# Two value projections run block by block as x arrives, with 1/rms applied after the projections

## The chip, the cores and the metric

The kernel runs on one core of a Trainium2 chip. The time is device microseconds for one execution, the median of several runs. The core has five engines that run side by side, each with its own instruction queue in a fixed order: TensorE (PE, matrix products into PSUM, with its weight loads shown apart as PEld), VectorE (DVE), ScalarE (ACT), GpSimd (POOL), and SyncE (SP), which issues most of the DMAs. Data moves from device memory to SBUF by DMA; PE reads SBUF and writes PSUM, which has eight banks of 128 x 512 float32.

## What is computed

One layer of a streaming encoder on x (512 x 1024, float32): a token mixer, cross-attention into 256 memory tokens, and a SwiGLU. Each has an RMSNorm before and after. The change touches only the first norm and the projections that read it:

```python
h = rms_norm(x, g_mix_pre[l])            # x * rsqrt(mean(x*x) + EPS) * g
proj = h @ w_in[l]                       # 1024 -> 3*512 + 8 + 3*512
q_f, k_f, v_f, f_logit, q_c, k_c, v_c = jnp.split(proj, splits, axis=-1)
log_f = jax.nn.log_sigmoid((f_logit + b_fgate[l]).astype(jnp.float32))
o_f = fox_attention(...)                 # 8 heads of 64, causal, with forget gates
o_c = chunked_rel_attention(...)         # 8 heads of 64, banded, with a learned bias
```

The factor 1/rms belongs to a row of x (a token), the gain g to a column. So the product of (x * g) with the weights, multiplied by the token's 1/rms afterwards, is the same projection.

## The kernel before

**Precision.** Every float32 matrix product is made of three products in a reduced format (fp32r). Each operand is split into hi (rounded by a ScalarE cast or activation) and lo (the rest, by a VectorE subtraction), and `mm3` (L137) adds hi x hi, hi x lo and lo x hi in PSUM.

**Weights.** All weights come through a list of units. A unit is a block of columns of one matrix (mostly 1024 x 256). `load_unit` (L97) issues its DMAs on SP into `raw` tiles (3 buffers), casts hi on ScalarE (L113), and subtracts lo on VectorE (L120) or, for three of four row blocks of the second half, on GpSimd (L116). There are two hi and two lo buffers. `unit()` (L130) hands out the next unit and starts the load of the one behind it.

**Opening.** x comes transposed (features on partitions) in 8 blocks of 128 features. `first_products` (L254) runs as pieces of the first unit (value columns of the second group of fox heads and the 8 forget logits, 264 columns) arrive, piece sizes 1, 1, 2, 2, 2 blocks: for each block it makes hTh and hTl from x * g (L266, L267) and issues 12 products into four PSUM banks `acc0`. It also squares x (L256) and adds up the squares (L258 on GpSimd, L262 and L263 on VectorE). `feature_rstd` (L235) sums them over partitions on PE (L239), takes the power -1/2 (L144, L145), and spreads it over a row of PSUM (L246): `rcol` has 1/rms per token as a column, `rrow` as a row. The four accumulators of the first value unit are copied to V with the factor `rcol` (`raw_v`, L286). Then the second value unit is projected from the same hTh and hTl, 8 blocks x 4 row tiles x 3 products (L305 to L312), and copied in the same way.

**Rescaling h.** While that second projection runs, L314 to L319 make the normalised h for all others: per block xs = x * g * rrow (L315, VectorE, reading rrow from PSUM), hTh again (L318, ScalarE), hTl again (L319, VectorE).

**Heads.** Four groups of four heads follow (two fox, two chunked). `group_proj` (L357) projects a group's values (the first two are there already, in `first_v`), queries and keys. `proj_blocks` (L339) makes two blocks of 128 columns x 512 tokens each; `fin_q` (L376) and `fin_k` (L390) split each block from PSUM into hi and lo for single heads. `head` (L479) is the attention of one head: scores on PE, a row minimum of the negated biased scores on VectorE (L492), exponential on ScalarE (L502), scaling (L503, L504), transposes on PE (L507), hi and lo of the result (L509, L510), and the product with V (L516). Projections of the next group and weight work of later stages lie between the steps of a head on PE; the order on each engine is fixed at build time by a planner that goes by program order, shifted by `later(n)`.

**PSUM.** The banks are shared by tags: a (3), s (2), t (2), o (1). `acc0` takes s, s, a, o; the second value projection takes a, a; statistics take t.

Of the kernel before, what the change touches and what calls it, by code (L numbers as in the profile page):

```python
# [8 lines left out]
F32 = mybir.dt.float32  # L9
F32R = mybir.dt.float32r  # L10
# [23 lines left out]
def hybrid_block_kernel(  # L34
# [44 lines left out]
    def gcol(c):  # L79
        return gn[:, c : c + 1]  # L80
# [16 lines left out]
    def load_unit(w, k0, nkb, c0, ncol, dst=None, sizes=None, after=None):  # L97
        u = len(loaded)
        if dst is None:
            hi = wp.tile([P, nkb, ncol], F32R, tag="hi", name=f"hi{u}", bufs=2)  # L100
            lo = wp.tile([P, nkb, ncol], F32R, tag="lo", name=f"lo{u}", bufs=2)
        else:
            hi, lo = dst()
        step = nkb if nkb * ncol <= 1024 else 4 if ncol < 512 else 2
        j = 0
        for n in sizes or [min(step, nkb - k) for k in range(0, nkb, step)]:
            raw = wp.tile([P, n, ncol], F32, tag="raw", name=f"raw{u}_{j}", bufs=3)
            r0 = (k0 + j) * P
# [4 lines left out]
            act.copy(hi[:, j : j + n, :], raw)  # L113
            pk = 0 if j == 0 or not 2 <= u < 26 else 3 if ncol == 256 else 2 if u >= 20 else 0
            if pk:
                pool.tensor_tensor(  # L116
                    out=lo[:, j : j + pk, :], in0=raw[:, :pk, :], in1=f32(hi[:, j : j + pk, :]), op=ALU.subtract
                )
            if pk < n:
                dve.tensor_tensor(  # L120
                    out=lo[:, j + pk : j + n, :], in0=raw[:, pk:, :], in1=f32(hi[:, j + pk : j + n, :]), op=ALU.subtract
                )
# [101 lines left out]
    with tc.tile_pool(name="mix", bufs=1, reuse_waits="tile") as bp:  # L224
# [3 lines left out]
        warm = small(1, "warm")  # L228
        act.activation(warm, ones, AF.Square)
        acc0 = [bank(tag) for tag in ("s", "s", "a", "o")]  # L230

        def load_x(k, n):
            nc.sync.dma_start(xt[:, k : k + n, :], x_t[k * P : (k + n) * P, :].rearrange("(k p) n -> p k n", p=P))

        def feature_rstd(sq, blocks, n, name):  # L235
            ss = bank("t")
# [11 lines left out]
                )  # L248
            return r, rb[:, : n * P]

        pieces = (1, 1, 2, 2, 2)
        stats = []

        def first_products(hi, lo, k0, n):  # L254
            def squares():
                act.activation(xs[:, k0 : k0 + n, :], xt[:, k0 : k0 + n, :], AF.Square, scale=1.0 / 32.0)  # L256
                for k in range(max(k0, 1), min(k0 + n, KB - 2)):
                    pool.tensor_tensor(out=xs[:, 0, :], in0=xs[:, 0, :], in1=xs[:, k, :], op=ALU.add)  # L258

            if k0 + n == KB:  # L260
                squares()
                dve.tensor_tensor(out=xs[:, KB - 2, :], in0=xs[:, KB - 2, :], in1=xs[:, KB - 1, :], op=ALU.add)  # L262
                dve.tensor_tensor(out=xs[:, 0, :], in0=xs[:, 0, :], in1=xs[:, KB - 2, :], op=ALU.add)  # L263
                stats.append(feature_rstd(xs, (0,), NT, "rx"))
            for k in range(k0, k0 + n):
                act.activation(hTh[:, k, :], xt[:, k, :], AF.Copy, scale=gcol(G_MIX + k))  # L266
                dve.scalar_tensor_tensor(  # L267
                    out=hTl[:, k, :], in0=xt[:, k, :], scalar=gcol(G_MIX + k), in1=f32(hTh[:, k, :]),
                    op0=ALU.mult, op1=ALU.subtract,
                )  # L270
                for t in range(NT):
                    ts = slice(t * P, (t + 1) * P)
                    mm3(acc0[t][:, :264], hTh[:, k, ts], hTl[:, k, ts], hi[:, k, :], lo[:, k, :], k == 0, k == KB - 1)
            if k0 + n < KB:
                load_x(k0 + n, 2 if k0 else 1)
                squares()

        load_x(0, 1)
        load_unit(*units[0], sizes=pieces, after=first_products)

        rcol, rrow = stats[0]

        def v_tile(name):
            return bp.tile([P, NT, 4, 128], F32R, tag="V", name=f"V{name}", bufs=2)
# [11 lines left out]
        for t in range(NT):  # L296
# [6 lines left out]
        acc1 = [bank("a"), bank("a")]  # L303
        load_unit(*units[1])
        for k in range(KB):  # L305
            for t in range(NT):
                ts = slice(t * P, (t + 1) * P)
                mm3(
                    acc1[t // 2][:, (t % 2) * 256 : (t % 2 + 1) * 256], hTh[:, k, ts], hTl[:, k, ts],
                    loaded[1][0][:, k, :], loaded[1][1][:, k, :],  # L310
                    k == 0 and t % 2 == 0, k == KB - 1 and t % 2 == 1,
                )  # L312
        used[0] = 2
        for k in range(KB):  # L314
            dve.scalar_tensor_tensor(  # L315
                out=xs[:, k, :], in0=xt[:, k, :], scalar=gcol(G_MIX + k), in1=rrow, op0=ALU.mult, op1=ALU.mult
            )
# [39 lines left out]
        def group_proj(name):  # L357
            q, kt, kl = [], [], []
            if first_v:
                v = first_v.pop(0)  # L360
            else:
                v = v_tile(name)
                hi, lo = unit()
                for t in range(NT):
                    ts = slice(t * P, (t + 1) * P)
                    if t % 2 == 0:
                        acc = bank("a")
                    a = acc[:, (t % 2) * 256 : (t % 2 + 1) * 256]
                    for k in range(KB):
                        mm3(a, hTh[:, k, ts], hTl[:, k, ts], hi[:, k, :], lo[:, k, :], k == 0, k == KB - 1)  # L370
                    if t % 2:
                        a4, vt = acc.rearrange("p (t h d) -> p t h d", t=2, h=4), v[:, t - 1 : t + 1]
                        act.copy(vt[..., 0:64], a4)
                        dve.tensor_tensor(out=vt[..., 64:128], in0=a4, in1=f32(vt[..., 0:64]), op=ALU.subtract)

            def fin_q(b, acc):  # L376
                t = bp.tile([P, 2, SEQ], F32R, tag="Q", name=f"Q{name}{b}", bufs=3)
                for h, own, other in ((0, H0, H1), (1, H1, H0)):
                    act.activation(t[own, h, :], acc[own, :], AF.Copy, scale=0.125)
                    dve.scalar_tensor_tensor(  # L380
                        out=t[other, h, :],
                        in0=acc[own, :],
                        scalar=0.125,
                        in1=f32(t[own, h, :]),
                        op0=ALU.mult,
                        op1=ALU.subtract,
                    )
                q.append(t)

            def fin_k(b, acc):  # L390
                t = bp.tile([P, 2, SEQ], F32R, tag="T", name=f"T{name}{b}", bufs=3)
                l = klz[nkl[0] % len(klz)]
                nkl[0] += 1
                for h, own, other in ((0, H0, H1), (1, H1, H0)):
                    act.copy(t[own, h, :], acc[own, :])
                    dve.tensor_tensor(
                        out=l[own, h, :], in0=acc[own, :], in1=f32(t[own, h, :]), op=ALU.subtract
                    )
# [509 lines left out]
```

## Time and profile before

| | |
|---|---|
| median of 3 runs | 821.29 us (820.76 to 821.74) |
| the profiled execution | 820.63 us, span 818.9 us |
| mean granted PE clock | 0.994 |
| instructions | 10498 |
| loads of x / of weights on SP (median, issue to landing) | 512 KB 6.6 us / 512 KB 3.8 us |

The profiled execution's own time is 1.7 us above its span, from the first to the last instruction. In the lines below, an engine's share is its busy time over the span; a timeline line has the start, the duration, engine, line of the kernel, operation, and in square brackets how long the engine stood idle before it and what released it. Groups have a count, the busy time, the mean duration in ns of one, and the idle time of their engine just before them.

### The profile page before, as it was taken

The numbers are of one execution on the slowest core, as the hardware profiler recorded it, in microseconds if no ns is written. First come the engines' busy times: TensorE is split into PE (matmuls) and PEld (weight loads), VectorE is DVE, ScalarE is ACT, GpSimd is POOL, SyncE is SP. The second block draws the span as 40 slices with busy tenths as digits, with TensorE's granted clock in tenths as the row PEclk, the third lists the DMA queues.
The fourth block names the chain that finished last, engine by engine and source line by source line (L and its number), as shares of the span: only waits on it lengthen the run. The fifth ranks groups of instructions, "written<-read, shape, count | busy, mean of one in ns | idle before, by whom it ended". The sixth has DMA issues, their size and how long they took to land.

```text
span 818.9 us, 10498 instructions
## 1 busy us (share of the span) xinstructions
PE 789.2 (96%) x4028; PEld 659.8 (81%) x4028; DVE 436.1 (53%) x784; ACT 375.2 (46%) x681; POOL 115.0 (14%) x133
## 2 busy tenths in 40 slices
PE   6999999999999988999999999999999999999996
PEld 5986787887779976877787988888888888888885
DVE  4877888669887579555635433333333333113214
ACT  7457888648875357444536432332333323113211
POOL 5112233220334153100011100000000000000001
PEclk9899999999999999999999999999999999999999
DMA  7151112332413824412403033333333332332312
GB/s 233 52 155 52 53 52 80 89 102 64 130 52 99 288 65 141 141 65 65 143 26 102 27 103 102 103 103 104 103 103 102 86 95 80 100 103 66 116 51 103
DMA packets 61794, 79.91 MB, mean 98 GB/s; under 512 B 2736, under 2 KB 45744, under 8 KB 61744
## 3 DMA queue, kind: packets, MB, share of 16 engines
q1 hardware_dynamic: 60320, 74.49, 29.5%
q0 software_dynamic: 1280, 4.72, 1.7%
q8 instruction: 32, 0.52, 0.3%
q14 instruction: 18, 0.15, 0.1%
q10 hardware_dynamic: 144, 0.02, 0.0%
HBM read 77.13 MB, written 2.10 MB: 97 GB/s over the span
## 4 chain that ended last, share of the span: by engine, by line
PE 77%; ACT 8%; DVE 8%; POOL 3%; issue 3%; DMA 1%; SPq 0%; DVEq 0%; POOLq 0%; ACTq 0%
PE ps_a L140 15%; PE ps_a L139 15%; PE ps_a L138 15%; PE ps_s L139 7%; PE ps_s L140 7%; PE ps_s L138 7%; ACT p L502 2%; DVE p L504 1%; PE ps_o L516 1%; PE ps_t L507 1%; DVE lo L120 1%; ACT fb L458 1%; ACT hi L113 1%; PE ps_o L138 1%; DVE p L492 1%
## 5 line engine op out<-in xcount | busy, mean ns | idle before, releaser
L120 DVE TENSOR_TENSOR lo<-raw,hi 128x1024 fp32r<-128x1024 f32 (+3 forms) x125 | 147.5, 1202 | 148.1 <-ACT hi L113 142.3
L113 ACT CAST hi<-raw 128x1024 fp32r<-128x1024 f32 (+2 forms) x129 | 129.3, 1030 | 181.9 <-PE ps_a L139 58.3
L140 PE MATMUL ps_a<-hTh,lo 128*128 128x512 f32 x192 | 76.3, 397 | 0.5 <-DVE lo L120 0.5
L138 PE MATMUL ps_a<-hTh,hi 128*128 128x512 f32 x192 | 76.3, 398 | 0.0
L139 PE MATMUL ps_a<-hTl,hi 128*128 128x512 f32 x192 | 75.8, 395 | 0.0
L139 PE MATMUL ps_s<-fl,hi 128*128 128x512 f32 (+1 forms) x192 | 71.6, 373 | 0.0
L138 PE MATMUL ps_s<-fh,hi 128*128 128x512 f32 (+1 forms) x192 | 71.6, 373 | 0.0
L140 PE MATMUL ps_s<-fh,lo 128*128 128x512 f32 (+1 forms) x192 | 71.5, 373 | 0.0
L139 PE MATMUL ps_a<-fl,hi 128*128 128x512 f32 (+1 forms) x192 | 71.5, 372 | 0.0
L140 PE MATMUL ps_a<-fh,lo 128*128 128x512 f32 (+1 forms) x192 | 71.4, 372 | 0.0
L138 PE MATMUL ps_a<-fh,hi 128*128 128x512 f32 (+1 forms) x192 | 71.4, 372 | 0.0
L805 DVE TENSOR_TENSOR silu<-silu,ps_s 128x512 f32<-128x512 f32 x22 | 15.1, 688 | 97.1 <-PE ps_s L140 97.1
L116 POOL TENSOR_TENSOR lo<-raw,hi 128x768 fp32r<-128x768 f32 (+1 forms) x20 | 43.0, 2150 | 114.8 <-ACT hi L113 114.8
L844 POOL TENSOR_TENSOR frs<-frs,mhalf 128x1 f32<-128x1 f32 x4 | 2.2, 543 | 356.1 <-DVE frs L843 356.1
L502 ACT ACTIVATE p<-p,nm 128x128 f32<-128x128 f32 (+1 forms) x64 | 36.1, 565 | 15.9 <-DVE nm L492 15.3
L140 PEld LDWEIGHTS ps_a<-hTh,lo 128*128 128x128 f32 x192 | 36.1, 188 | 7.3 <-DVE lo L120 0.9
L138 PEld LDWEIGHTS ps_s<-fh,hi 128*128 128x128 f32 x192 | 36.2, 189 | 6.3
L140 PEld LDWEIGHTS ps_a<-fh,lo 128*128 128x128 f32 x192 | 36.2, 189 | 6.3
L139 PEld LDWEIGHTS ps_a<-fl,hi 128*128 128x128 f32 x192 | 36.1, 188 | 6.2
L138 PEld LDWEIGHTS ps_a<-fh,hi 128*128 128x128 f32 x192 | 36.1, 188 | 6.3
L140 PEld LDWEIGHTS ps_s<-fh,lo 128*128 128x128 f32 x192 | 36.1, 188 | 6.2
L139 PEld LDWEIGHTS ps_s<-fl,hi 128*128 128x128 f32 x192 | 36.2, 188 | 6.1
(274 smaller groups left out, 1861.8 us busy)
## 6 DMA issues: line engine op xcount, KB each, us to landing
raw<-in_dram SPq DMA_DIRECT2D x128, 512.0 KB, 3.8
cb<-in_dram SPq DMA_DIRECT2D x8, 256.0 KB, 2.6
xo<-in_dram POOLq DMA_DIRECT2D x4, 512.0 KB, 7.4
out_dram<-yd SPq DMA_DIRECT2D x8, 256.0 KB, 2.1
xt<-in_dram SPq DMA_DIRECT2D x3, 512.0 KB, 6.6
gb<-in_dram POOLq DMA_DIRECT2D x3, 512.0 KB, 4.1
mm<-in_dram POOLq DMA_DIRECT2D x1, 1024.0 KB, 6.2
raw<-in_dram SPq DMA_DIRECT2D x3, 264.0 KB, 5.8
```

Of the source, the lines that this page charges most:

```text
L113: act.copy(hi[:, j : j + n, :], raw)
L116: pool.tensor_tensor(out=lo[:, j : j + pk, :], in0=raw[:, :pk, :], in1=f32(hi[:, j : j + pk, :]), op=ALU.subtract)
L120: dve.tensor_tensor(out=lo[:, j + pk : j + n, :], in0=raw[:, pk:, :], in1=f32(hi[:, j + pk : j + n, :]), op=ALU.subtract)
L138: pe.matmul(dst, sh, mh, start=first, stop=False)
L139: pe.matmul(dst, sh, ml, start=False, stop=False)
L140: pe.matmul(dst, sl, mh, start=False, stop=last)
L458: act.activation(t[:, :n], acc[:, :n], AF.Identity, bias=ct[:, i, h : h + 1])
L492: dve.tensor_tensor_reduce(out=p[:, :n], in0=s[:, :n], in1=bias[i], scale=-1.0, scalar=BIG, op0=ALU.add, op1=ALU.min, accum_out=nm,)
L502: act.activation(p[:, :n], p[:, :n], AF.Exp, bias=nm, scale=-1.0, accum_out=sm)
L504: dve.tensor_scalar(out=p[:, :n], in0=p[:, :n], scalar1=rs, scalar2=None, op0=ALU.mult)
L507: pe.transpose(tp[:, k * P : (k + 1) * P], p[:, k * P : (k + 1) * P], ident)
L805: dve.tensor_tensor(out=s, in0=s, in1=ua, op=ALU.mult)
```

## The change

- The first two value units leave the list of units. `load_v` loads both column ranges (520 columns) of one or two blocks in one DMA. `v_weights` splits them into two pairs of hi and lo tiles, which occupy both buffers of each kind; for block 0 the cast is on VectorE instead of ScalarE.
- For each block, `x_block` makes hTh and hTl from x * g as before, and `v_products` issues the 12 products of the first unit and the 12 of the second, into `acc0` and `acc1` together.
- The first eight DMAs are issued in a row: x and weights of blocks 0, 1 and 2-3, then x of blocks 4-5 and 6-7. The weights of blocks 4-5 and 6-7 come as `raw` buffers become free.
- The squares of blocks 4 to 7 are taken while blocks 2 and 3 are in work; the statistics are issued on PE after block 5. `rrow` is copied from PSUM to an SBUF tile.
- The rescaling of h (L314 to L319) is gone. hTh and hTl stay x * g for all projections. Each query or key block is multiplied by `rrow` on its way out of PSUM into an SBUF tile `scaled` (2 buffers), from which `fin_q` and `fin_k` read. Value blocks of the two chunked groups are copied by `raw_v` with `rcol`, one row tile at a time.
- Six products of a zeroed tile, whose result nobody reads, are issued on PE at the start.
- The scratch for DMAs issued by GpSimd is 4096 instead of 8192. The bounds for GpSimd's share of the lo work are shifted by the two units that left the list, so that the same units are shared as before.

```diff
+    rrow = cst.tile([P, SEQ], F32, tag="rrow", name="rrow")
+    still = rrow[:, :P]
+    dve.memset(still, 0.0)
...
-            pk = 0 if j == 0 or not 2 <= u < 26 else 3 if ncol == 256 else 2 if u >= 20 else 0
+            pk = 0 if j == 0 or not 0 <= u < 24 else 3 if ncol == 256 else 2 if u >= 18 else 0
...
-    units.insert(1, units.pop(3))
+    del units[3], units[0]
...
+        acc1 = [bank("a"), bank("a")]
+        warmed = bank("t")
+        for j in range(6):
+            pe.matmul(warmed[:, :P], still, still, start=True, stop=True)
...
+        def load_v(k, n):
+            raw = wp.tile([P, n, 520], F32, tag="raw", name=f"rawv{k}", bufs=3)
+            nc.sync.dma_start(raw, w_in[k * P : (k + n) * P, 1024:1544].rearrange("(k p) n -> p k n", p=P))
+            return raw
...
+        vhi = [wp.tile([P, KB, n], F32R, tag="hi", name=f"vhi{n}", bufs=2) for n in (264, 256)]
+        vlo = [wp.tile([P, KB, n], F32R, tag="lo", name=f"vlo{n}", bufs=2) for n in (264, 256)]
+        halves = (slice(256, 520), slice(0, 256))
+
+        def v_weights(raw, k, n):
+            for j, cs in enumerate(halves):
+                h = vhi[j][:, k : k + n, :]
+                if k == 0:
+                    dve.tensor_copy(h, raw[:, :, cs])
+                else:
+                    act.copy(h, raw[:, :, cs])
+            for j, cs in enumerate(halves):
+                dve.tensor_tensor(
+                    out=vlo[j][:, k : k + n, :], in0=raw[:, :, cs], in1=f32(vhi[j][:, k : k + n, :]), op=ALU.subtract
+                )
...
+        def squares(k, n):
+            act.activation(xs[:, k : k + n, :], xt[:, k : k + n, :], AF.Square, scale=1.0 / 32.0)
+            for j in range(max(k, 1), min(k + n, KB - 2)):
+                pool.tensor_tensor(out=xs[:, 0, :], in0=xs[:, 0, :], in1=xs[:, j, :], op=ALU.add)
+
+        def v_products(k):
+            for t in range(NT):
+                ts = slice(t * P, (t + 1) * P)
+                mm3(acc0[t][:, :264], hTh[:, k, ts], hTl[:, k, ts], vhi[0][:, k, :], vlo[0][:, k, :], k == 0, k == KB - 1)
+            for t in range(NT):
+                ts = slice(t * P, (t + 1) * P)
+                mm3(
+                    acc1[t // 2][:, (t % 2) * 256 : (t % 2 + 1) * 256], hTh[:, k, ts], hTl[:, k, ts],
+                    vhi[1][:, k, :], vlo[1][:, k, :], k == 0 and t % 2 == 0, k == KB - 1 and t % 2 == 1,
+                )
+
+        load_x(0, 1)
+        raws = {0: load_v(0, 1)}
+        load_x(1, 1)
+        raws[1] = load_v(1, 1)
+        load_x(2, 2)
+        raws[2] = load_v(2, 2)
+        load_x(4, 2)
+        load_x(6, 2)
+        for k, n in ((0, 1), (1, 1), (2, 2), (4, 2), (6, 2)):
+            if k not in raws:
+                raws[k] = load_v(k, n)
+            for j in range(k, k + n):
+                x_block(j)
+            v_weights(raws[k], k, n)
+            if k < 4:
+                squares(k, n)
+            if k == 2:
+                squares(4, 2)
+                squares(6, 2)
                 dve.tensor_tensor(out=xs[:, KB - 2, :], in0=xs[:, KB - 2, :], in1=xs[:, KB - 1, :], op=ALU.add)
                 dve.tensor_tensor(out=xs[:, 0, :], in0=xs[:, 0, :], in1=xs[:, KB - 2, :], op=ALU.add)
...
+            for j in range(k, k + n):
+                v_products(j)
+            if k == 4:
+                rcol, rps = feature_rstd(xs, (0,), NT, "rx")
+                act.copy(rrow, rps)
...
-        for k in range(KB):
-            dve.scalar_tensor_tensor(
-                out=xs[:, k, :], in0=xt[:, k, :], scalar=gcol(G_MIX + k), in1=rrow, op0=ALU.mult, op1=ALU.mult
-            )
-            act.copy(hTh[:, k, :], xs[:, k, :])
-            dve.tensor_tensor(out=hTl[:, k, :], in0=xs[:, k, :], in1=f32(hTh[:, k, :]), op=ALU.subtract)
...
-                finish(b, acc)
+                scaled = bp.tile([P, SEQ], F32, tag="qk", name="qk", bufs=2)
+                dve.tensor_tensor(out=scaled, in0=acc, in1=rrow, op=ALU.mult)
+                finish(b, scaled)
...
-                    if t % 2:
-                        a4, vt = acc.rearrange("p (t h d) -> p t h d", t=2, h=4), v[:, t - 1 : t + 1]
-                        act.copy(vt[..., 0:64], a4)
-                        dve.tensor_tensor(out=vt[..., 64:128], in0=a4, in1=f32(vt[..., 0:64]), op=ALU.subtract)
+                    raw_v(v, t, a, rcol[:, t : t + 1])
...
-    nc = _bacc.Bacc("TRN2", target_bir_lowering=False, num_devices=1, dynamic_dma_scratch_size=8192)
+    nc = _bacc.Bacc("TRN2", target_bir_lowering=False, num_devices=1, dynamic_dma_scratch_size=4096)
```

More of the change, by code (lines that the diff above doesn't have):

```diff
@@ L249, in feature_rstd @@
             return r, rb[:, : n * P]
[L251 to L261, printed above, removed]
+        vhi = [wp.tile([P, KB, n], F32R, tag="hi", name=f"vhi{n}", bufs=2) for n in (264, 256)]
@@ new lines, in x_block @@
+        def x_block(k):
+            act.activation(hTh[:, k, :], xt[:, k, :], AF.Copy, scale=gcol(G_MIX + k))
+            dve.scalar_tensor_tensor(
+                out=hTl[:, k, :], in0=xt[:, k, :], scalar=gcol(G_MIX + k), in1=f32(hTh[:, k, :]),
+                op0=ALU.mult, op1=ALU.subtract,
+            )
[3 more added lines that the diff above has]
+                pool.tensor_tensor(out=xs[:, 0, :], in0=xs[:, 0, :], in1=xs[:, j, :], op=ALU.add)
@@ new lines, in v_products @@
+        def v_products(k):
[7 more added lines that the diff above has]
+                    vhi[1][:, k, :], vlo[1][:, k, :], k == 0 and t % 2 == 0, k == KB - 1 and t % 2 == 1,
+                )
@@ L262, in first_products @@
                 dve.tensor_tensor(out=xs[:, KB - 2, :], in0=xs[:, KB - 2, :], in1=xs[:, KB - 1, :], op=ALU.add)
                 dve.tensor_tensor(out=xs[:, 0, :], in0=xs[:, 0, :], in1=xs[:, KB - 2, :], op=ALU.add)
[L264 to L269, printed above, removed]
-                )
-                for t in range(NT):
-                    ts = slice(t * P, (t + 1) * P)
-                    mm3(acc0[t][:, :264], hTh[:, k, ts], hTl[:, k, ts], hi[:, k, :], lo[:, k, :], k == 0, k == KB - 1)
@@ L274, in first_products @@
[L274 to L281, printed above, removed]
+            for j in range(k, k + n):
[3 more added lines that the diff above has]
+                act.copy(rrow, rps)
         def v_tile(name):
@@ L302, in hybrid_block_kernel @@
             )
-        acc1 = [bank("a"), bank("a")]
-        load_unit(*units[1])
-        for k in range(KB):
[L306 to L315, printed above, removed]
-                out=xs[:, k, :], in0=xt[:, k, :], scalar=gcol(G_MIX + k), in1=rrow, op0=ALU.mult, op1=ALU.mult
-            )
-            act.copy(hTh[:, k, :], xs[:, k, :])
-            dve.tensor_tensor(out=hTl[:, k, :], in0=xs[:, k, :], in1=f32(hTh[:, k, :]), op=ALU.subtract)
         for t in range(NT):
```

## The prediction

> **What bounds the kernel now.** I read the page first, then busy time by stretches of the span, then the waits of TensorE and the timeline of the opening.
>
> ```profile
> span 818.9 us, 10498 instructions
> PE 789.2 (96%) x4028; PEld 659.8 (81%) x4028; DVE 436.1 (53%) x784; ACT 375.2 (46%) x681; POOL 115.0 (14%) x133
> PE 77%; ACT 8%; DVE 8%; POOL 3%; issue 3%; DMA 1%; SPq 0%; DVEq 0%; POOLq 0%; ACTq 0%
> ```
>
> TensorE (PE) is busy 96% of the span and carries 77% of the chain that ended last. So the change can win only where PE stands idle or runs at a low clock, or lose by making PE wait. The stretches say where:
>
> ```profile
> 0.00:8.00 8.00, 2.93 (x12) 2.78 (x13) 1.98 (x6) 4.25 (x8) 0.83 (x7) 1.00 0.71 223
> 8.00:15.00 7.00, 6.61 (x44) 5.98 (x43) 5.15 (x7) 6.62 (x10) 5.81 (x9) 1.00 0.82 276
> 15.00:20.00 5.00, 2.88 (x23) 2.63 (x22) 2.20 (x3) 4.06 (x6) 4.89 (x8) 0.98 0.71 189
> 20.00:25.00 5.00, 3.93 (x16) 3.62 (x17) 3.66 (x6) 0.00 (x0) 1.99 (x4) 0.50 0.07 25
> 25.00:40.00 15.00, 15.00 (x120) 15.00 (x119) 12.80 (x24) 7.92 (x16) 1.85 (x1) 0.94 0.24 70
> ```
>
> Columns: stretch, its length, busy time of PE, weight loads, VectorE (DVE), ScalarE (ACT) and GpSimd (POOL), granted clock, DMA share, GB/s. PE is busy 2.9 of the first 8 us and 2.9 of 5 us from 15 on, and from 20 to 25 the granted clock is 0.50. The timeline of PE shows the events:
>
> ```profile
> 5.07 0.81 PE L138 MATMUL ps_s<-hi,hTh 128*128 128x264 f32 x2 [5.07 <-ACT hi L113]
> 9.28 0.42 PE L139 MATMUL ps_s<-lo,hTh 128*128 128x264 f32 x1
> 9.67 0.28 PE L138 MATMUL ps_a<-hi,hTh 128*128 128x264 f32 x1
> 20.80 1.86 PE L239 MATMUL ps_t<-ones,xs 128*128 128x1 f32 x8 [2.92 <-DVE xs L263]
> 24.46 2.07 PE L246 MATMUL ps_t<-ident,rx 128*128 128x128 f32 x8 [0.27 <-POOL rx L145]
> 26.73 0.28 PE L140 MATMUL ps_o<-hi,hTl 128*128 128x264 f32 x1
> 28.30 0.28 PE L138 MATMUL ps_a<-hi,hTh 128*128 128x256 f32 x1
> 39.69 0.28 PE L140 MATMUL ps_a<-hi,hTl 128*128 128x256 f32 x1
> 39.81 0.40 PE L138 MATMUL ps_a<-hTh,hi 128*128 128x512 f32 x1
> 40.90 0.50 PE L140 MATMUL ps_a<-hTh,lo 128*128 128x512 f32 x1 [0.46 <-DVE lo L120]
> ```
>
> The two value projections are 192 products (8 blocks x 4 row tiles x 3, twice). From 28.30 to 39.69 the second one's 96 start 0.120 us apart (11.39/95): the pace at full clock. Up to about 9.5 us a product takes 0.42 us, and 0.28 after it: the opening is at half clock. At 20.80 PE has stood 2.92 us for the mean squares. At full pace 192 products need 23.0 us; they take 34.7 (5.07 to 39.81). Some 11.7 us in front of the first query product are therefore the room of this change.
>
> **The change part by part.**
>
> *Both value projections per block.* The loads of x and of 520 weight columns are 0.53 MB a block, 1.9 us at the 276 GB/s of 8 to 15 us (a rate that held waits of the queue, so a lower bound of the speed). PE needs 24 x 0.120 = 2.9 us for a block: once running, PE is the bound, not DMA. The early arrivals:
>
> ```profile
> 7.52 0.41 ACT L113 CAST hi<-raw 128x264 fp32r<-128x264 f32 x1 [0.46 <-DMA raw<-in_dram]
> 8.84 1.34 ACT L266 ACTIVATE hTh<-xt,gn 128x512 fp32r<-128x512 f32 x2 [0.38 <-DMA xt<-in_dram]
> L113 ACT CAST hi<-raw 128x528 fp32r<-128x528 f32 x3 | 1.9, 618 | 0.0
> L120 DVE TENSOR_TENSOR lo<-raw,hi 128x528 fp32r<-128x528 f32 x3 | 2.1, 694 | 0.0
> ```
>
> At 7.52 us 0.79 MB had landed, at 8.84 us 1.32 MB. Block 0's weights come 0.13 MB later than now: 0.6 us at 223 GB/s, so PE starts at 5.7. Block 1 is complete at 1.06 MB, about 8.2, and cast by 8.6, which is when block 0 ends (5.7 + 2.9). Blocks 2 and 3 are complete at 2.11 MB: 8.84 + 0.79/0.276 = 11.7, with the cast of 0.62 about 12.3, and lo needs 0.69 more; PE would be free at 11.5. I take 0.8 us of waits (bounds 0, and 2.5 if lo stands in the way each time). ScalarE's and VectorE's work for a block (cast, x block, squares) is below 2 us by these rows and hides under 2.9. On SP all eight first DMAs issue without a wait; the loads of blocks 4 and 6 wait for a raw buffer freed by blocks 0 and 1 (7 to 10 us), while more than 1 MB still stands in the queue ahead of them: nothing.
>
> *Statistics.* Their matmuls (1.86 + 2.07 us at clock 0.50) come when PE has products to do, so the 2.92 us of waiting go and they run at full clock: 2.0 us (upper bound 3.9). POOL's five additions lie beside it. The squares of blocks 4 to 7 now stand ahead of block 4's work on ScalarE, 2 x 1.05 us while PE works on blocks 2 and 3.
>
> *Six warm-up products on zeros.* By L246, where 4 products make 8 records of 0.26 us, they are some 3 us of work, and PE has nothing to do before 5: free. What they save lies between 0 and the 2.0 us now lost between 5.7 and 9.5. No row shows the clock after such products; I leave 0.8 us as lost.
>
> The Trainium skill (TensorE: Matmul & The Clock Gate, Part 1) says that the gate opens after a busy window of about 3.4 us whose phase is free-running, so an estimate by that page is that 3 us of warm-up may or may not fill one. The trace agrees in kind: one opening at 9.5 us, 4.4 us after the first product, one some 5.9 us after 20.80.
>
> The last value product then ends at 5.7 + 23.0 + 2.0 + 0.8 + 0.8 = 32.3 instead of 39.8: **7.5 us gained** (bounds 9.1 with no clock loss and no wait; 2.7 with 3.9, 2.0 and 2.5).
>
> *The first query weights.* Two hi and two lo buffers exist and both value units now hold them to the end. The first query hi can be cast only after the last product of the first value unit, 12 products (1.4 us) before the end.
>
> ```profile
> L113 ACT CAST hi<-raw 128x1024 fp32r<-128x1024 f32 x5 | 5.1, 1055 | 0.0
> L120 DVE TENSOR_TENSOR lo<-raw,hi 128x1024 fp32r<-128x1024 f32 x3 | 3.6, 1213 | 0.0
> L289 DVE SCALAR_TENSOR_TENSOR V<-ps_a,rx,V 128x256 fp32r<-128x256 f32 x2 | 0.9, 472 | 0.0
> ```
>
> Cast 1.06 and lo 1.21 are 2.3 us after it, with a V copy or two (0.47) in front: PE waits about 1.3 us where it now waits 0.46. **0.8 us lost** (bounds 0; 2.8 if all eight copies go first).
>
> *The rescaling of h.* Eight each of L315, L318 and L319 go. They lie under the second value projection, where PE never waits; by themselves they give nothing beyond the 0.46 above. In return each of 16 query and key blocks gets a VectorE multiplication out of PSUM, and the operations that split a block into hi and lo (two of VectorE's each) read SBUF instead of PSUM.
>
> ```profile
> L315 DVE SCALAR_TENSOR_TENSOR xs<-xt,gn,ps_t 128x512 f32<-128x512 f32 x8 | 5.5, 736 | 0.0
> L396 DVE TENSOR_TENSOR L<-ps_a,T 64x512 fp32r<-64x512 f32 x15 | 10.3, 686 | 3.3 <-ACT T L395 3.1
> L529 DVE SCALAR_TENSOR_TENSOR ol<-o,gn,oh 128x512 fp32r<-128x512 f32 x7 | 6.4, 909 | 0.6 <-ACT oh L528 0.5
> L267 DVE SCALAR_TENSOR_TENSOR hTl<-xt,gn,hTh x8: 739/752/1776, 4.7 to 22.8; 128x512 fp32r<-128x512 f32 x8
> L374 DVE TENSOR_TENSOR V<-ps_a,V 128x512 fp32r<-128x512 f32 x4 | 2.7, 683 | 1.0 <-ACT V L373 1.0
> ```
>
> The multiplication is about 0.69 us (L396, one PSUM source). Four fall into the first group's projections, where VectorE has room; twelve, 8.3 us, into the attention. There the same kind of operation with both sources in SBUF (L529) averages 909 ns against 739 undisturbed (the least of L267): 0.17 us more, for 24 splits 4.1 us. The V copies of two groups grow from 4 x 0.68 to 8 x 0.47: 1.0 us. Together **13.4 us more on VectorE** among the heads. What of it reaches PE:
>
> ```profile
> 72.00:100.00 28.00, 26.15 (x133) 20.17 (x134) 23.57 (x71) 23.77 (x59) 6.52 (x14) 1.00 0.14 38
> 100.00:140.00 40.00, 38.48 (x249) 34.01 (x248) 34.61 (x98) 35.73 (x87) 11.68 (x21) 1.00 0.23 62
> ...
> sum 168.00, PE 161.92 PEld 134.88 DVE 137.91 ACT 129.27 POOL 43.98; mean PE 40.48 PEld 33.72 DVE 34.48 ACT 32.32 POOL 10.99
> PE ps_t L507 <- DVE p L504: 4.5, 7, 1.1
> PE ps_s L488 <- DVE nm L492: 1.6, 3, 1.1
> ```
>
> From 72 to 240 PE is idle 6.1 us, and its waits (56 to 240) name VectorE for 6.1. If these grow with VectorE's load (13.4/137.9) it is 0.6 us; if with the loss of its free time (30.1 to 16.7) it is 4.9. **I take 2.0**, nearer the first, since the projections of the next group fill PE while a head waits. Ends: 0, and 13.4 were VectorE the bound. Below zero is excluded: accumulators come free earlier, but no wait for one is among PE's.
>
> *The smaller DMA scratch* touches only the loads issued by GpSimd, of which the first in need is that of the memory:
>
> ```profile
> L569 POOL DMA_DIRECT2D mm<-in_dram x1: 1118/1118/1118, 209.5 to 209.5; - x1
> L573 ACT ACTIVATE msq<-mm x4: 624/630/636, 217.1 to 224.7; 128x512 f32<-128x512 f32 x4
> DMA to landing us min/median/max: 6.2/6.2/6.2
> ```
>
> It lands at 215.7 and is read at 217.1. No row shows a smaller scratch: 0, or 4.8 us of ScalarE waiting if the landing took twice as long, which PE's other work there would largely cover. I take nothing.
>
> **Sum.** -7.5 + 0.8 + 2.0 = -4.7 on the profiled execution's 820.63 us (span 818.9 and 1.7 around it; the median of the runs is 821.29): **815.9 us**.
>
> **Rivals.**
> - *The attention hides it all* and the query wait is no longer than now: 820.63 - 7.5 = 813.1. For it: 96% busy PE there, 18% free VectorE. Against: every PE wait there names VectorE.
> - *The warm-up does not open the gate*: 1.2 us more, 817.1. For it: the pause between the zeros and the first product (about 4.3 to 5.7). Against: the clock opened at 9.5 after a start with similar gaps.
> - *VectorE becomes the bound of the heads* (slower): all 13.4 reach the end, 820.63 - 7.5 + 0.8 + 13.4 = 827.3. It decides once more than half of the 13.4 (6.7 us) lands on the chain of a head. For it: 82% load, 86% and more from 72 to 140 (58.2 of 68 us). Against: ScalarE is as loaded there, and after 240 PE has no wait at all.
> - *The opening is won and given back about evenly*: 819.7 to 822.9.
>
> Beside the third rival stands a page: the Trainium skill (SBUF — State Buffer, SBUF: two separate sides) says that GpSimd and a VectorE operation with two SBUF inputs exclude each other for a whole instruction. By L529 against L396 the trace agrees; that speaks against moving 32 splits from PSUM to SBUF.
>
> **How the numbers follow.** Forecast 0.50, all hidden 0.20, no warm-up 0.11, given back 0.09, VectorE bound 0.10. About 0.2% (1.6 us) can be told from no change in this kernel: faster 0.81, within it 0.09, slower 0.10. The range runs from 812.0 (between all hidden and the 9.1 bound) to 819.6, leaving out the last two rivals.
>
> **What would show it.** Right: first query product near 32 to 34 us, no PE wait of 2.9 us and no clock of 0.50 after 10; PE's idle time among the heads up from 6 to about 8 us; splits undisturbed by GpSimd near 0.69 us and blocked ones above 1. Wrong: PE waits on casts for every block before 20 us, or PE idle among the heads above 13 us with VectorE named.

## The result: slower by half a per cent

| | before | after |
|---|---|---|
| median, us | 821.51 (820.76 to 822.38) | 825.91 (825.07 to 826.51) |
| ratio of the times | | 1.0052, 95% interval 1.0035 to 1.0070 |
| the profiled execution, us | 820.63, span 818.9 | 825.32, span 823.5 |
| first query product starts, us | 39.81 | 35.31 |
| first transpose of a head's weights, us | 72.73 | 70.98 |
| last transpose of a head's weights, us | 247.0 | 245.2 |
| first gate or up product of the SwiGLU, us | 448.57 | 446.62 |
| first down product, us | 692.28 | 695.69 |

The forecast was 815.9 us, and the measured time lies far above its range. The start times in the table, read from the timeline of TensorE, say where. (One execution of e7 below, 2016.73 us, and one of e8, 874.67 us, were slow ones and count in no ratio.) The change does what it was forecast to do, though less of it: the first query product starts 4.5 us earlier, and the SwiGLU still starts 2.0 us earlier. Then the kernel loses 5.4 us in a stage whose code the change does not touch: gate and up take 249.07 us instead of 243.71. The down products and what follows them cost another 1.2 us (127.8 against 126.6).

The page of the changed kernel:

```profile
span 823.5 us, 10512 instructions
PE 798.5 (97%) x4040; PEld 659.3 (80%) x4040; DVE 438.0 (53%) x794; ACT 372.8 (45%) x679; POOL 117.5 (14%) x133
PE 80%; DVE 6%; ACT 5%; issue 2%; POOL 2%; DMA 1%; DVEq 0%; POOLq 0%; ACTq 0%
```

TensorE is busy 9.3 us more than before (789.2), of which the zeros (12 records) are 2.9. A busy TensorE that takes longer for the same products is what the page shows. The busy time of a long stretch of gate and up, 500 to 600 us, first before, then after (columns as in the prediction):

```profile
500.00:600.00 100.00, 100.00 (x442) 82.80 (x442) 31.39 (x35) 26.38 (x35) 0.00 (x0) 1.00 0.31 95
```

```profile
500.00:600.00 100.00, 100.00 (x430) 80.58 (x429) 30.95 (x34) 26.04 (x34) 0.00 (x0) 1.00 0.29 89
```

TensorE never stands idle in either, and the granted clock is 1.00 in both. In the same 100 us it starts 442 products before and 430 after. No wait, no DMA and no clock tells them apart: each product takes longer. The timeline of TensorE, of before and then of after, thirteen products in a row:

```profile
559.68 0.39 PE L138 MATMUL ps_s<-fh,hi 128*128 128x512 f32 x1
...
562.40 0.39 PE L138 MATMUL ps_a<-fh,hi 128*128 128x512 f32 x1
```

```profile
559.66 0.40 PE L143 MATMUL ps_s<-fh,lo 128*128 128x512 f32 x1
...
562.46 0.40 PE L143 MATMUL ps_a<-fh,lo 128*128 128x512 f32 x1
```

Twelve steps of 0.227 us in the one, of 0.233 in the other. The groups of TensorE by shape show which products are touched. First before, then after (count, busy time, mean ns of one):

```profile
L138 PE MATMUL ps_a<-fh,hi 128*128 128x512 f32 x160 | 62.3, 389 | 0.0
L138 PE MATMUL ps_a<-woh,oTh 128*128 128x512 f32 x32 | 12.8, 401 | 0.0
```

```profile
L141 PE MATMUL ps_a<-fh,hi 128*128 128x512 f32 x160 | 63.3, 395 | 0.0
L141 PE MATMUL ps_a<-woh,oTh 128*128 128x512 f32 x32 | 12.8, 401 | 0.0
```

The gate and up products (weights `hi`, moving operand `fh`) are slower by 6 ns. Products of the same shape with `woh` and `oTh` are not, which speaks against the chip or the run and for something in the operands.

**The theory.** The larger loads of the change need larger tiles: a `raw` buffer holds 2 blocks of 520 columns, 4160 bytes a partition, where it held 4096. Three such buffers are 192 bytes more, and every pool behind them lies 192 bytes further from the weight buffers in front of them. In the compiled programs `hi` begins at byte 10656 of a partition and `hTh` at 56736 before, which is 180 x 256 bytes apart. After, they begin at 8608 and 54880: the distance is no multiple of 256, and `hi` minus `hTh`, divided by 256, leaves a remainder of 64. `woh`, `wol` and `oTh` moved together, and theirs is unchanged.

I matched each product in the traces with the addresses in the compiled programs, and grouped the time from one product's start to the next one's by a distance: the address of the weights that are loaded for the next product, less that of the operand that moves through now, modulo 256 (the remainder after division by 256). The table has mean and count for products behind 28 us; remainders that occur once are left out, and the rows "0" of after belong to products whose distance did not change. Of the 153 wide ones there, the same kinds take 229.8 in before, so half of what they lie above 227.7 is no effect of the change.

```
kernel    distance mod 256   512 columns: count, mean ns   256 columns: count, mean ns
before            0               2426   227.7                 767   119.6
after             0                153   231.9                 147   119.4
after            64               1427   233.3                 355   113.7
after           192                846   229.4                 190   116.6
```

For after's counts this is 1427 x 5.6 + 846 x 1.7 ns = 9.4 us less 355 x 5.9 + 190 x 3.0 ns = 2.7 us, so 6.7 us in all. Between the first gate product and the first down product alone it is 959 steps of 226.7 that became 233.3 (+6.4 us) and 170 of 119.7 that became 113.8 (-1.0), together +5.4: all that the stage lost.

**The rivals.** One is that the new code itself slows the chip down, by more work of VectorE and GpSimd; but in 500 to 600 us both engines do as much as before. The other is that the pace follows the absolute place of a tile, not a distance. The first five experiments decide.

### The profile page after: what moved, and what is told of

It is laid out like the page before. It is cut to its first block, busy times and chain, and to the rows that moved or that the text cites. A ratio compares the mean times of both kernels' runs of the same rounds, so it can differ in the third digit from the quotient of the medians.

```text
span 823.5 us, 10512 instructions
## 1 busy us (share of the span) xinstructions
PE 798.5 (97%) x4040; PEld 659.3 (80%) x4040; DVE 438.0 (53%) x794; ACT 372.8 (45%) x679; POOL 117.5 (14%) x133
## 4 chain that ended last, share of the span: by engine, by line
PE 80%; DVE 6%; ACT 5%; issue 2%; POOL 2%; DMA 1%; DVEq 0%; POOLq 0%; ACTq 0%
PE ps_a L143 16%; PE ps_a L141 16%; PE ps_a L142 16%; PE ps_s L142 7%; PE ps_s L143 7%; PE ps_s L141 7%; PE ps_t L534 2%; DVE lo L123 2%; PE ps_o L543 1%; PE ps_o L141 1%; PE ps_t L143 1%; DVE p L531 1%; PE ps_t L142 1%; PE ps_s L515 1%; PE ps_o L142 1%
## 5 line engine op out<-in xcount | busy, mean ns | idle before, releaser
L123 DVE TENSOR_TENSOR lo<-raw,hi 128x1024 fp32r<-128x1024 f32 x118 | 145.4, 1256 | 145.3 <-ACT hi L116 144.2
L116 ACT CAST hi<-raw 128x1024 fp32r<-128x1024 f32 x122 | 124.3, 1048 | 186.3 <-PE ps_a L142 55.8
L119 POOL TENSOR_TENSOR lo<-raw,hi 128x768 fp32r<-128x768 f32 (+1 forms) x20 | 45.1, 2255 | 96.9 <-ACT hi L116 93.8
L141 PEld LDWEIGHTS ps_a<-hTh,hi 128*128 128x128 f32 x192 | 36.2, 188 | 7.0 <-ACT hi L116 0.4
```

What stands on the lines that cost most here:

```text
L119: pool.tensor_tensor(out=lo[:, j : j + pk, :], in0=raw[:, :pk, :], in1=f32(hi[:, j : j + pk, :]), op=ALU.subtract)
L123: dve.tensor_tensor(out=lo[:, j + pk : j + n, :], in0=raw[:, pk:, :], in1=f32(hi[:, j + pk : j + n, :]), op=ALU.subtract)
L141: pe.matmul(dst, sh, mh, start=first, stop=False)
```

## Experiments

Where a median of before stands below, it comes from runs on the same chip. "A tile" that is added is set to zero once and not read by anything.

### The placement alone, in both directions

e1 is the kernel before with 192 unused bytes in the pool of the weights, behind the `raw` tiles. e2 is the changed kernel with 64 unused bytes at the same place, which makes the 192 of the change 256. The edit of e1, which in e2 has 16 in place of 48:

```diff
+        gap = wp.tile([P, 48], F32, tag="gap", name="gap", bufs=1)
+        dve.memset(gap, 0.0)
```

> The kernel before with an unused 192-byte tile behind the raw buffers, so that hTh and every tile behind it lie 192 bytes further from the hi and lo weights, as in the changed kernel; nothing else differs but one small memset. Placement theory (the start-to-start time of PE's products depends on the distance between the moving operand and the weights loaded meanwhile, modulo 256 bytes): 512-column products of gate and up 233 ns apart instead of 227, 256-column ones 114 to 117 instead of 120; by the counts of the changed kernel's trace +8.0 +1.4 -2.1 -0.6 us, so about 828 us. Rival (the loss comes from the changed order of work or from VectorE's added work): 821.5 us, 227 ns.

> The changed kernel with a 64-byte tile behind the raw buffers, which brings the distance back to a multiple of 256 bytes. Placement theory: gate and up products 227 ns apart, 825.9 - 6.7 = about 819 us, a little faster than before. Rival (order of work or VectorE): 825.9 us, 233 ns.

e1 takes 829.13 us against 821.07, ratio 1.0101 (1.0087 to 1.0115). e2 takes 818.28, ratio 0.9968 (0.9955 to 0.9980). The stretch of 500 to 600 us in e1, and then in e2:

```profile
500.00:600.00 100.00, 100.00 (x430) 80.60 (x429) 33.03 (x36) 27.55 (x36) 0.00 (x0) 1.00 0.32 98
```

```profile
500.00:600.00 100.00, 100.00 (x443) 82.84 (x442) 32.55 (x36) 28.26 (x37) 0.00 (x0) 1.00 0.29 88
```

Nothing but bytes that nobody reads makes the kernel before lose 12 products per 100 us, and gives the changed kernel 13 back. In e1 the remainders 64 and 192 occur as in after, with nearly the same means (233.3 and 229.5), and by its own counts the table's reckoning gives 7.1 of its 8.1 us; the last microsecond is not traced. In e2 the distance is 0 again, and the mean 227.6. So the slower pace is shown to come from the placement, and the change of the computation by itself is faster than before, by 0.3%.

### Which placement

e3, e8 and e10 are e2 with other sizes of the unused tile: 192, 320 and 96 bytes instead of 64.

> The changed kernel with a 192-byte tile behind the raw buffers: the distance is then 128 bytes modulo 256, which neither trace has. Placement theory: a pace other than those of 0, 64 and 192, the same in all products of one width whichever operand is the moving one (128 and -128 are the same); the size is open. Rival: 825.9 us and the pace of the changed kernel.

> The changed kernel with a 320-byte tile, 256 bytes more than the 64-byte version. If only the distance modulo 256 counts: 818.3 us as that one, products 227 ns apart. If the modulus is 512 or more, or the absolute place counts: another time and pace.

> After with 96 unused bytes behind the raw tiles: the moving operands lie 32 bytes off the place of e2, at a distance to the weights that is no multiple of 64. Theory (the pace of the products hangs on the distance of the weights being loaded to the moving operand, modulo 256 bytes): this distance was in no run so far; a pace of 512-column products between that of its neighbours, 227.7 ns (distance 0) and 229 to 233 ns (64 and 192), some 228 to 233, and 818.5 to 826. Rival (only the place of whole 64-byte pieces counts, not where within them an operand begins): 227.7 ns as in e2, 818.3. A pace above 233.3 ns would say that operands across the edges of such pieces cost by themselves: above 829.

```
kernel   unused bytes   distances mod 256   512 columns, mean ns   time us   ratio (95% interval)
e2             64            0                 227.6                818.28    0.9968 (0.9955 to 0.9980)
e8            320            0                 227.7                818.46    0.9964 (0.9952 to 0.9977)
e10            96          224, 32             233.2, 233.3         828.97    1.0098 (1.0082 to 1.0113)
e3            192          128                 232.8                829.05    1.0106 (1.0088 to 1.0123)
```

Everything behind the weights lies 256 bytes further in e8 than in e2, and nothing changes: what counts, counts modulo 256 (at most). That it is the distance and not the place modulo 256 of one operand, the other products show. The 80 wide ones with `woh` or `wol` moving, whose weights `oTh` and `oTl` moved along with them, take 227.5 ns before, 228.7 after and a median of 227 in both. The wide ones of the down projection in which `hi` moves, itself at the same place modulo 256 in all these kernels, take 226.8 before, 229.5 after, 232.3 in e3 and 233.3 in e10. A shift of 32 bytes already costs as much as any other, so it is not whole pieces of 64 bytes that count. For e10 the theory had given a pace between those of its neighbours; it came out at the upper end, for both of its distances, and the time is 3 us above what was expected. Wide products lose at every distance but 0, from 1.7 to 5.6 ns. (The distances 64 and 224 come from products in which an activation such as `hTh` or `fh` moves, 192 and 32 from those in which a weight tile does; only 128 occurs in both, at 233.3 ns with `fh` moving and 232.3 with `hi`.) Products of 256 columns do not: they take 119.6 at 0, 119.0 at 128, 118.2 at 32, 116.7 at 224, 116.6 at 192 and 113.7 at 64.

What in the chip makes it so, the runs do not show. The Trainium skill (SBUF — State Buffer, Who interferes with whom) gives TensorE two read ports that are independent of one another, one for the moving operand and one for the weights. By that rule a distance between the two operands would change nothing; here it is worth 2.5% of each wide product, and the measurement decides.

### Each part of the change alone, at distance 0

Beside e2, which has both parts, e5 has the first: the two value projections together, but then h is rescaled in place as before and nothing is multiplied out of PSUM. e6 has the second: the opening of the kernel before, and 1/rms applied as projections leave PSUM.

The edit of e5, on e2:

```diff
+        for k in range(KB):
+            dve.scalar_tensor_tensor(out=xs[:, k, :], in0=xt[:, k, :], scalar=gcol(G_MIX + k), in1=rrow, op0=ALU.mult, op1=ALU.mult)
+            act.copy(hTh[:, k, :], xs[:, k, :])
+            dve.tensor_tensor(out=hTl[:, k, :], in0=xs[:, k, :], in1=f32(hTh[:, k, :]), op=ALU.subtract)
...
-                dve.tensor_tensor(out=scaled, in0=acc, in1=rrow, op=ALU.mult)
-                finish(b, scaled)
+                finish(b, acc)
```

and of e6, on before (the copies of the value blocks with `rcol` come along in e6, and go in e5):

```diff
-        for k in range(KB):
...
-                finish(b, acc)
+                dve.tensor_tensor(out=scaled, in0=acc, in1=rrow, op=ALU.mult)
+                finish(b, scaled)
```

> The 64-byte version with h rescaled in place again (the three operations per block, after the last value product) and query, key and value blocks split straight from PSUM: the combined opening alone. VectorE then has 8 x 1.4 us between the last value product (35 us) and the last query block, of which PE's own 5.4 us of query products hide half: +6 us; the heads lose what the multiplications cost them, -2 us. So about 822 us, and the first query products spread over some 11 us. If the multiplications cost the heads more than I think (6 us or more), the time is 818 or below.

> The kernel before with 1/rms applied as the projections leave PSUM, its opening and its placement (distance a multiple of 256 bytes) kept: the second part of the change alone. If the multiplications cost the heads 2 us: 821.1 + 2.0 - 0.4 for the query wait that goes = 822.7 us. If they cost nothing: 820.7. If VectorE were the bound of the heads: 830 or more.

e5 takes 828.50 us, ratio 1.0087 (1.0074 to 1.0100): 6.5 us more than I expected. TensorE's waits, VectorE's timeline, and busy times of e5:

```profile
PE ps_a L143 <- DVE lo L123: 9.5, 1, 9.5
```

```profile
35.84 3.63 DVE L350 SCALAR_TENSOR_TENSOR xs<-xt,gn,rrow 128x512 f32<-128x512 f32 x3
39.40 1.88 DVE L354 TENSOR_TENSOR hTl<-xs,hTh 128x512 fp32r<-128x512 f32 x3
...
44.13 1.21 DVE L123 TENSOR_TENSOR lo<-raw,hi 128x1024 fp32r<-128x1024 f32 x1
```

```profile
40.00:60.00 20.00, 14.61 (x52) 11.84 (x53) 11.77 (x25) 7.51 (x14) 2.10 (x1) 0.72 0.35 105
```

Little is left to cover the rescaling, because both value projections are nearly done: it begins at 29.94 us, the last value product starts at 34.29, and five of the eight blocks come behind it. They stand in VectorE's queue ahead of the low parts of the first query weights, and TensorE waits 9.5 us for these. Behind the pause its products start 0.43 us apart up to 51.1 us, against 0.23 from then on; the granted clock of 0.72 is the mean over the pause and what follows.

e6 takes 822.40 against 821.44, ratio 1.0016 (1.0007 to 1.0025): by itself the second part costs about 1 us. So the two parts are +7.1 and +1.0 us alone and -2.8 together (medians, each against before on its own chip). The second part is the price of the first: it takes away the rescaling that the first would lay bare.

### The zeros ahead of the opening

e4 is e2 without the six products of zeros, e7 is e2 with ten of them.

```diff
-        for j in range(6):
+        for j in range(10):
```

> As the 64-byte version, without the six products of the zeroed tile. If they help the clock (they are meant to open the gate before the first real product): the half clock lasts longer and the time is up to 2 us above the 64-byte version. If they do nothing, since the changed kernel's clock rose only at 11.7 us, against 9.6 before: the same time within 0.5 us. If they delay it: faster by up to 1 us.

> The 64-byte version with ten instead of six products of the zeroed tile, which then last until about 6 us, so that PE has no pause before the first real product (0.2 us later than now). If the gate opens after an unbroken busy stretch, whatever the operands: full clock from 5 to 8 us on and stays, up to 1.5 us faster than the 64-byte version. If zeros don't count: the same or 0.2 us slower.

e4 takes 818.36 (ratio 0.9967, 0.9955 to 0.9980) and e7 818.47 (0.9967, 0.9956 to 0.9978): like e2 both. In the profiled executions the clock does differ. The timeline of e2 shows products 0.12 us apart from 6.11 to 7.2, then 0.21 apart to 10.7, as if the zeros had been taken into account and then the pause behind them:

```profile
1.05 2.93 PE L237 MATMUL ps_t<-rrow 128*128 128x128 f32 x12 [1.05 <-DVE gap L353]
5.79 0.48 PE L141 MATMUL ps_s<-vhi,hTh 128*128 128x264 f32 x2 [1.80 <-DVE vhi L271]
...
7.76 0.42 PE L143 MATMUL ps_a<-vhi,hTl 128*128 128x256 f32 x1
7.98 0.41 PE L141 MATMUL ps_a<-vhi,hTh 128*128 128x256 f32 x1
```

```profile
7.20:10.80 3.60, 3.60 (x20) 3.60 (x19) 3.13 (x5) 2.95 (x6) 1.97 (x6) 0.53 1.04 386
```

In after the same six zeros leave the products 0.21 us apart to 11.64, and in e4, without zeros, they are 0.22 apart to 10.69. Ten zeros reach to the first product without a pause, and in that execution it is at full pace almost at once (20 records from 1.05 to 5.69, then 38 starts from 5 to 10 us where e2 has 20 in 3.6). Its first query product starts at 34.69 instead of 35.38 (35.24 in e4), but this 0.7 us is not seen in the medians, whose runs scatter by 2 us. Whether the zeros are worth anything stays open; it is less than these runs can tell.

### A wait of the opening

In e2 TensorE waits 1.5 us at 19 us, and in e7 1.7, for the low part of the fifth block's weights (`vlo`). The timelines of TensorE and VectorE in e7 say why:

```profile
20.02 0.39 PE L142 MATMUL ps_s<-vlo,hTh 128*128 128x264 f32 x1 [1.73 <-DVE vlo L275]
...
18.65 0.69 DVE L322 TENSOR_TENSOR xs<-xs 128x512 f32<-128x512 f32 x1 [2.89 <-POOL xs L289]
19.26 1.30 DVE L275 TENSOR_TENSOR vlo<-rawv,vhi 128x528 fp32r<-128x528 f32 x2
```

The last addition of squares waits 2.89 us for GpSimd's five, and `vlo` stands behind it in VectorE's queue. The earlier the clock is full, the longer this wait: 0.5 us in after, 0.7 in e4, 1.5 in e2, 1.7 in e7. It takes back a good part of what the zeros gain. e9 is e7 with that addition on GpSimd.

```diff
-                dve.tensor_tensor(out=xs[:, 0, :], in0=xs[:, 0, :], in1=xs[:, KB - 2, :], op=ALU.add)
+                pool.tensor_tensor(out=xs[:, 0, :], in0=xs[:, 0, :], in1=xs[:, KB - 2, :], op=ALU.add)
```

> The kernel of e7 (after, 64 unused bytes behind the raw tiles, ten zero products) with one change: the last addition of squares of the statistics, which waits for GpSimd's additions at the head of VectorE's queue, is issued on GpSimd itself. Theory (VectorE's queue holds the low parts of the next value blocks behind an instruction that waits for GpSimd): TensorE's wait of about 1.6 us at 19 us for a low part goes, the first query product starts at about 33.2 us instead of 34.7, and the time is about 1.5 us below that of e7 (818.5), 817.0. Rival (what is gained comes back: the reciprocal of the root mean square is later, the transpose of the statistics and the first query weights wait for it instead): the first query product at 34.5 to 35, time 818.2 to 818.7.

It takes 818.62 us (ratio 0.9971, 0.9960 to 0.9982), no gain. The time and the first query product (34.77 us, against 34.69 in e7) are the rival's, but not the rival's way. The timelines of VectorE, GpSimd and TensorE in e9:

```profile
17.51 3.97 DVE L275 TENSOR_TENSOR vlo<-rawv,vhi 128x528 fp32r<-128x528 f32 x2
...
17.47 1.27 POOL L289 TENSOR_TENSOR xs<-xs 128x512 f32<-128x512 f32 x1
...
19.65 1.28 POOL L322 TENSOR_TENSOR xs<-xs 128x512 f32<-128x512 f32 x1
...
19.37 0.39 PE L142 MATMUL ps_s<-vlo,hTh 128*128 128x264 f32 x1 [0.96 <-DVE vlo L275]
21.54 0.39 PE L142 MATMUL ps_a<-vlo,hTh 128*128 128x256 f32 x1 [0.43 <-DVE vlo L275]
```

`vlo` begins 1.75 us earlier, but two of them take 3.97 us instead of 1.30, beside GpSimd's additions. TensorE's wait of 1.73 becomes 0.96 + 0.43. One wait was exchanged for another: by the records each of the two subtractions overlaps one of GpSimd's additions and ends some 0.6 us behind it. That they share an access to SBUF would explain it, but no run tests that.

## Why the prediction was wrong, step by step

**The step that failed** is the sum. It took "-7.5 + 0.8 + 2.0" off the profiled execution's 820.63 us and so held every product behind the heads at its old duration, 0.227 us. In the part that lists what the change adds, the larger DMA of 520 columns was priced as a transfer only. That its tile is 64 bytes larger, and that this moves all pools behind it against the weights, is no term of the sum and no rival; it measures +6.7 us by the paces and 7.2 us between after and e2, each taken against before in its own comparison (4.40 + 2.79; 7.63 straight from 825.91 to 818.28). The trace of before held no row by which this could have been priced, since its wide products are all at distance 0; but that the operands move could be seen in the diff, and the bounds should have said so.

**The rivals.** The measured 825.91 is near the 827.3 of "VectorE becomes the bound of the heads", and that is a coincidence. Between 72 and 240 us, after:

```profile
72.00:240.00 168.00, 161.86 (x925) 133.53 (x924) 143.02 (x390) 129.41 (x299) 46.19 (x61) 1.00 0.24 73
```

TensorE stands idle 6.1 us there, as before, though VectorE is busy 5.1 us more, so the heads were not bound by it. (That this idle time would grow to 8 us, as the prediction's test had it, is wrong as well; where the heads do lose is shown below.)

The other steps can be judged by e2, where the distance is 0: 818.28, so -2.8 against 821.1 on that chip's runs (0.9968), where -4.7 had been forecast.

**The opening** was to end at 32.3 us and ended near 34.9 (half a microsecond ahead of the first query product), in after and in e2. The timeline of TensorE, after:

```profile
5.64 0.78 PE L141 MATMUL ps_s<-vhi,hTh 128*128 128x264 f32 x2 [1.66 <-DVE vhi L271]
...
11.42 0.41 PE L143 MATMUL ps_s<-vhi,hTl 128*128 128x264 f32 x1
11.64 0.31 PE L141 MATMUL ps_s<-vhi,hTh 128*128 128x264 f32 x1
...
20.71 0.39 PE L142 MATMUL ps_s<-vlo,hTh 128*128 128x264 f32 x1 [0.51 <-DVE vlo L275]
...
26.43 0.95 PE L251 MATMUL ps_t<-ones,xs 128*128 128x1 f32 x8
28.75 1.16 PE L258 MATMUL ps_t<-ident,rx 128*128 128x128 f32 x8 [0.77 <-POOL rx L148]
35.31 0.50 PE L141 MATMUL ps_a<-hTh,hi 128*128 128x512 f32 x1 [0.19 <-ACT hi L116]
36.65 0.50 PE L143 MATMUL ps_a<-hTh,lo 128*128 128x512 f32 x1 [0.60 <-DVE lo L123]
```

- The start, 5.7, was right (5.64), and so were the statistics, 2.0 us (0.95 + 1.16).
- The clock was mis-sized. From 5.64 to 11.64 products start 0.21 us apart, half the full pace, so 3.0 us are lost where 0.8 had been taken. In e2 it is half of 7.2 to 10.7, 1.7 us.
- The waits of 0.8 us were right in size (0.5 in after, 1.5 in e2) and wrong in kind. The prediction worked them out from late loads and had the low parts only in its upper bound; here VectorE's queue is held by GpSimd's additions of squares, which the prediction had "beside" the work.
- A wait of 0.77 us between the two halves of the statistics, for GpSimd's power, was in no term.
- Together 2.2 - 0.3 + 0.8 = 2.7 us, which is the difference but for 0.1.

**The first query weights** cost 0.19 + 0.60 where 0.46 stood before, 0.3 us instead of 0.8.

**The heads** were to cost 2.0 us, and do. The lead of a kernel over before is how much earlier it has started the same amount of moved columns on TensorE, zeros not counted:

```
at us                     60    140    200    230    260    440    500    690
e2 (both parts)          4.2    5.0    4.1    2.2    2.2    2.5    2.5    2.5
e6 (second part alone)   0.4    1.1    0.1   -1.9   -1.9   -2.8   -2.8   -2.8
after                    3.7    4.6    3.8    1.8    2.2    1.9    2.2   -3.4
```

Until 200 us the projections of the next group cover the longer chain of a head, as was argued; the last heads have none, and 2.0 us (e2) and 2.3 us (e6, from 60 to 230) are lost. For the same products (206.16 to 227.91 us in e2, 210.19 to 230.10 in before) TensorE's idle time grows from 0.2 to 1.3 us; where the rest goes is not traced. By the medians e6 costs only 1.0 us, or 1.4 with the 0.4 that it has gained by 60 us, so 2.0 is the figure of single executions. That it meets the forecast is in part luck, since the way to this number was not all right. The rows of VectorE in after:

```profile
L375 DVE TENSOR_TENSOR qk<-ps_a,rrow 128x512 f32<-128x512 f32 x16 | 10.9, 684 | 5.1 <-PE ps_a L143 5.0
L407 DVE SCALAR_TENSOR_TENSOR Q<-qk,Q 64x512 fp32r<-64x512 f32 x16 | 11.0, 686 | 1.1 <-ACT Q L406 0.7
L423 DVE TENSOR_TENSOR L<-qk,T 64x512 fp32r<-64x512 f32 x16 | 11.0, 684 | 4.3 <-ACT T L422 4.2
```

The multiplication takes the 0.69 us that were taken. The splits, now with both sources in SBUF, take 0.69 as before and not 0.91: the 4.1 us for meeting GpSimd there did not come, and the slow L529 on which they rested is no rule for these splits. And one wait for an accumulator did, which had been excluded, as TensorE's waits from 56 to 240 us show:

```profile
PE ps_t L534 <- DVE p L531: 4.2, 6, 1.1
PE ps_s L515 <- DVE nm L519: 1.1, 1, 1.1
PE ps_a L141 <- DVE V L335: 1.0, 1, 1.0
```

**The smaller DMA scratch** cost nothing: the memory still lands 6.2 us after its issue.

So without the placement the forecast would have been 2.3 us too low, by the profiled executions (818.28 in e2 against 815.9): 2.7 too much from the opening, 0.4 too much taken for the query weights. 818.3 is inside its range, and the forecast's sign would have held.

## What to carry to other kernels

When a change alters the size of any tile, write down how far everything behind it moves, and compare the pace of untouched products, from start to start over a row of them, before looking for waits: a busy engine that does fewer products per 100 us is not explained by the chain of waits. Here the changed kernel with 64 unused bytes (e2) takes 818.3 us against 821.1 for before on the same chip, and 320 bytes (e8) do as well; a comparison that leaves such bytes to chance can turn a gain of 0.3% into a loss of 0.5%. When two parts of a change are tried one at a time, each may lose and both together win.

## What the runs showed of the hardware that was not expected

- A step between these fp32r products of 512 columns takes 227.7 ns when weights and moving operand lie a multiple of 256 bytes apart, and 229.4 to 233.3 at the five other distances seen (32, 64, 128, 192, 224); one of 256 columns takes 119.6 and 113.7 to 119.0.
- Two subtractions of VectorE took 3.97 us beside two additions of GpSimd (e9), and 1.30 us without them (e7).
- After a pause the clock can fall in one execution and not in another. In after, TensorE waits 2.73 us at 304.6, and the products behind it run at a granted clock of 0.53 for 3.6 us; e2's trace has the same pause (2.78 us) and no such stretch. Of the others, e3, e4, e8 and e9 have it as well, and before, e7 and e10 have only the pause.

```profile
304.59 0.98 PE L167 MATMUL ps_t<-ident,xo 128*128 128x128 f32 x6 [2.73 <-ACT xo L156]
```

```profile
305.00:308.60 3.60, 3.60 (x13) 2.92 (x12) 2.66 (x6) 3.60 (x8) 0.54 (x1) 0.53 0.39 150
```
